# Second products of an expert's odd last bin: both k halves and both column halves side by side, one-hot transposes to match

## The chip, the cores and the metric

One core of a Trainium2 chip runs the program. The metric is device microseconds of one execution, the median of several runs. The engines that matter here are TensorE (its matmuls are "PE" in the profile, its weight loads "PEld"), VectorE (DVE), ScalarE (ACT) and the DMA queues: q1 carries data, q8 carries the program text of an engine.

## The reference, cut to what matters

A two-layer encoder for 256 tokens of width 1024. Its last stage is a mixture of eight experts, and the change lies there:

```
gate = sum(one_hot(top_idx, 8) * softmax(top_logit))      # two experts for each token
out = 0
for e in range(8):
    out += gate[:, e] * ((silu(x @ w1[e]) * (x @ w3[e])) @ w2[e])
```

w1 and w3 are 1024 x 3584, w2 is 3584 x 1024, all float32. The inputs are fixed, so the number of tokens of each expert is fixed too: 61, 32, 101, 73, 49, 83, 23, 90.

## The kernel before, in words

An expert's tokens are gathered into up to 128 columns, cut into **bins** of 32. The experts 0 to 7 so have 2, 1, 4, 3, 2, 3, 1 and 3 bins, 19 in all. TensorE works through the bins with a 32-column stationary operand, and so uses one of four column groups of the array; a product therefore goes to one **quarter** (32 partitions) of a PSUM tile, and four products that write four quarters run side by side.

The expert's weights come as 42 **blocks** of 1 MB, 128 x 2048 floats. Blocks 0 to 27 are the first products (w1, w3), blocks 28 to 41 the second products (w2): such a second block holds two k tiles (index `i`) of 128 rows by 1024 columns, the columns in two halves (`half`). Method `second(j)` (line 914) multiplies block 28 + j. Its inner `pair(m)` (line 919) does the bins 2m and 2m+1: for each i, each half and each bin rr one product of 512 columns into quarter 2 * half + rr of `py[m]`, 8 products in all, which add up over i:

```
for i in range(2):
    for half in range(2):
        for rr in range(2):
            g = 2 * half + rr
```

So a bin's two halves of the columns sit in two quarters, and a pair that has one bin only still does 8 products, 4 of them on a bin without tokens.

How many bins an expert has is known only on the chip. Before the experts, the counts are compared with 32.5, 64.5 and 96.5 and loaded into registers of TensorE alone (`sel`). `bins_over(n, some, none)` (line 841) is a branch on such a register; both branches are in the program, one after the other, and the other engines pass them with an unconditional branch. `second` calls `pair(0)`, then `bins_over(2, ...)` round `pair(1)`; where the second pair isn't there, a tiny matmul `mark` (line 824) takes its place. `quad` (line 851) does the first products in the same way, with a branch for each bin.

`where` (line 947) transposes the one-hot matrix of the expert's places, 16 small matmuls (line 952); `add` (line 967) multiplies these transposes with the second products and so brings the rows back to the tokens, in two column halves.

The order of the work is written out by hand in `moe` (lines 985 to 1039): for an expert the blocks 0 to 7, then the last two second blocks of the expert before, then blocks 8 to 23, second blocks 0 to 3, the gather for the next expert, blocks 24 to 27, and second blocks 4 to 11, with the transposes (`turn`, line 898) and `where` between. The blocks are fetched by SP's queue in this order into a ring of about 21 places, so that a block's transfer waits until TensorE has used the place's last block.

Of the kernel before, what the change touches and what calls it, by code (L numbers as in the profile page):

```python
# [21 lines left out]
D = 1024  # L22
# [49 lines left out]
def trunk(tc, A, out):  # L72
    nc = tc.nc
# [573 lines left out]
    def moe(xs, gb):  # L647
        with tc.tile_pool(name="moe", bufs=1, reuse_waits="tile") as ep:
# [48 lines left out]
            zero = ep.tile([128, 512], BF16, name="zero")  # L697
# [124 lines left out]
            def mark(ps):  # L822

                nc.tensor.matmul(ps[0:32, 0:1], zero[:, 0:32], zero[:, 0:1], start=True, stop=True)  # L824

            class Expert:
# [90 lines left out]
                def second(self, j):  # L917

                    w, q, c = self.w[28 + j], j // 4, j % 4

                    def pair(m):
                        for i in range(2):
                            for half in range(2):
                                for rr in range(2):
                                    g = 2 * half + rr
                                    if q < 3:
                                        h = self.h[q][m][:, rr, i, 32 * c:32 * c + 32]
                                    else:
                                        h = self.h[q][0][:, m, i, 32 * (2 * rr + c):32 * (2 * rr + c) + 32]
                                    nc.tensor.matmul(self.py[m][32 * g:32 * g + 32], h,  # L930
                                                     w[:, i * D + half * 512:i * D + half * 512 + 512],
                                                     start=j == 0 and i == 0, stop=j == 13 and i == 1)

                    def zeros():
                        if j:
                            mark(self.py[1])
                        else:
                            nc.tensor.matmul(self.py[1], zero[:, 0:128], zero, start=True, stop=True)

                    pair(0)  # L940
                    self.bins_over(2, lambda: pair(1), zeros)

                def where_places(self):
                    self.wtr = trp.tile([128, 2, 2, 128], F32, name="tr")

                def where(self):

                    for m in range(2):
                        for t in range(2):
                            for g in range(4):  # L950
                                r = 2 * m + g % 2
                                nc.tensor.matmul(self.wtr[32 * g:32 * g + 32, m, t], self.oh[:, t, 32 * r:32 * r + 32],
                                                 ident, start=True, stop=True)

                def wheres(self):
                    self.ohT = (xhp if self.inner else ep).tile([128, 2, 2, 128], F32R, name="ohT",
                                                                tag="xl" if self.inner else "ohT")
                    nc.scalar.activation(self.ohT, self.wtr, AF.Copy)
# [99 lines left out]
            with tc.manual_schedule():  # L1058
# [6 lines left out]
                for t in range(2):  # L1065
                    for h in range(2):
                        c = norms[t].finish(h)
# [11 lines left out]
    for l in range(DEPTH):  # L1079
        xs = mixer(l, xs, lambda l=l: load_gb(1 + 2 * l))  # L1080
        if l % 2 == 0:
            xs = ffn(xs, lambda: load_gb(2))
    moe(xs, lambda: load_gb(4))
    ctx.close()

# [145 lines left out]
```

## Time and profile before

| | us |
|---|---|
| median of three runs | 1604.64 (1604.07 to 1605.26) |
| the profiled execution, its own time | 1606.61 |
| its span, from the first to the last instruction | 1604.6 |
| experts, from their first product to the last | 672.6 to 1586 |
| PE busy over the span | 1539.1 (96%) |
| DVE, ACT busy over the span | 574.3 (36%), 427.7 (27%) |

The profiled execution has 2.0 us outside its span, and is 2.0 us slower than the median. Read PE's 96% with care: the matmuls of four quarters overlap, and the busy time of an engine that waits in the middle of such a group can look full. What the experts' stage is held up by is read from its waits, expert by expert.

The order in which TensorE's instructions stand, from the listing of the built program (x8 is eight products in a row; the program holds the branches one after the other). On TensorE, a second block before (L930 is `pair`, L824 `mark`; `s` is py, `raw` the block, `eh` the hidden values):

```order
L930 MATMUL s<-raw,eh 32x512 x8
L845 COMPARE_AND_BRANCH
L930 MATMUL s<-raw,eh 32x512 x8
L845 UNCONDITIONAL_BRANCH
L824 LDWEIGHTS zero
L824 MATMUL s<-zero 32x1
L845 UNCONDITIONAL_BRANCH
```

The second pair and the mark are the two ways of one branch, after a first pair that is always done.

### The profile page before, as it was taken

What the parts mean: (1) busy time and instruction counts of PE and PEld (TensorE: products, weight loads), DVE (VectorE), ACT (ScalarE), POOL (GpSimd) and SP (SyncE); (2) the same over time, 40 slices, a digit from 0 to 9 for tenths busy, and PEclk for the clock granted to TensorE, in tenths of its full rate; (3) what the DMA queues carried; (4) which work ended last, traced back from release to release, by engine and by line L of the source; (5) the groups of instructions that cost most, each with busy time, mean ns of one, the idle gap of its engine ahead of it and who ended that gap; (6) DMA issues with size and microseconds to landing.
All of it is one profiled execution on the core that took longest, in us unless ns stands there. A gap on an engine that the chain in (4) does not pass through costs nothing. (4 is left out here: it accounts for less than half of the span.)

```text
span 1604.6 us, 27197 instructions
## 1 busy us (share of the span) xinstructions
PE 1539.1 (96%) x11516; PEld 861.4 (54%) x11533; DVE 574.3 (36%) x1070; ACT 427.7 (27%) x704; POOL 28.7 (2%) x29
## 2 busy tenths in 40 slices
PE   8999999999999999899799999999999999999996
PEld 7687887888786877634232333433334343334332
DVE  7689576554676967510110100110010200210102
ACT  4556555444364666210010000000000100110001
POOL 1000000000010000000000000000000000000000
PEclk9999999999999999999899999999999999999998
DMA  8444546555454564799999999997999997999930
GB/s 348 152 138 158 190 157 221 184 189 193 161 187 165 180 247 161 282 419 418 417 419 420 419 420 350 369 342 273 345 418 419 419 414 281 401 419 419 419 127 29
DMA packets 66977, 468.95 MB, mean 292 GB/s; under 512 B 7552, under 2 KB 8192, under 8 KB 11264
## 3 DMA queue, kind: packets, MB, share of 16 engines
q1 hardware_dynamic: 66816, 466.55, 74.6%
q8 instruction: 131, 2.15, 0.5%
q14 instruction: 30, 0.25, 0.0%
HBM read 465.48 MB, written 1.05 MB: 291 GB/s over the span
## 5 line engine op out<-in xcount | busy, mean ns | idle before, releaser
L858 PE MATMUL mm<-raw,xe 128*32 128x512 f32 x4416 | 499.8, 598 | 20.2 <-issue 13.9
L171 PE MATMUL mm<-w,xh 128*128 128x512 f32 (+2 forms) x1184 | 313.7, 385 | 1.9 <-ACT xh L163 1.9
L858 PEld LDWEIGHTS mm<-raw,xe 128*32 128x32 f32 x4416 | 164.8, 110 | 267.0 <-issue 241.3
L930 PE MATMUL s<-raw,eh 128*32 128x512 f32 x2688 | 300.2, 595 | 6.3 <-DMA raw<-wmoe 4.6
L139 DVE TENSOR_TENSOR w<-raw,w 128x1024 fp32r<-128x1024 f32 (+1 forms) x198 | 238.4, 1208 | 135.4 <-ACT w L135 134.7
L135 ACT ACTIVATE w<-raw 128x1024 fp32r<-128x1024 f32 (+1 forms) x198 | 206.2, 1047 | 198.7 <-PE mm L171 172.6
L171 PEld LDWEIGHTS mm<-w,xh 128*128 128x128 f32 x1184 | 215.7, 189 | 45.7 <-ACT xh L163 3.6
L930 PEld LDWEIGHTS s<-raw,eh 128*32 128x32 f32 x2688 | 92.5, 110 | 175.9 <-issue 158.2
L171 PE MATMUL mm<-w,xl 128*128 128x512 f32 (+2 forms) x592 | 178.1, 384 | 0.6 <-DVE xl L164 0.6
L911 ACT ACTIVATE eh<-tr 128x512 f32<-128x512 f32 x32 | 19.1, 597 | 494.9 <-PE tr L901 494.9
L892 DVE TENSOR_TENSOR fs<-mm,fs 128x256 f32<-128x256 f32 x112 | 40.4, 416 | 284.0 <-ACT fs L891 283.9
L909 DVE COPY eh<-tr 128x512 f32<-128x512 f32 x24 | 16.6, 692 | 294.1 <-PE tr L901 294.1
L171 PEld LDWEIGHTS mm<-w,xl 128*128 128x128 f32 x592 | 107.9, 189 | 22.2 <-issue 1.5
L891 ACT ACTIVATE fs<-mm 128x256 f32<-128x256 f32 x112 | 34.9, 393 | 202.1 <-PE mm L858 175.5
L824 PEld LDWEIGHTS <-zero 128*32 128x32 bf16 x211 | 20.7, 98 | 80.3 <-issue 80.3
L978 DVE SCALAR_TENSOR_TENSOR acc<-tr,egate,acc 128x512 f32<-128x512 f32 x32 | 22.8, 749 | 106.1 <-PE tr L974 106.1
L520 DVE SCALAR_TENSOR_TENSOR ac<-ud,smc,ac 128x256 f32<-128x256 f32 x120 | 53.2, 479 | 0.7
L171 PE MATMUL mm<-xh,w 128*128 128x256 f32 x256 | 45.2, 289 | 0.0
L171 PE MATMUL mm<-w,hh 128*128 128x512 f32 x144 | 44.3, 389 | 0.0
L171 PEld LDWEIGHTS mm<-xh,w 128*128 128x128 f32 x256 | 36.3, 191 | 3.2 <-issue 3.0
L171 PE MATMUL mm<-w,yh 128*128 128x512 f32 x128 | 35.8, 401 | 0.0
L824 PE MATMUL mm<-zero 128*32 128x1 bf16 x159 | 26.8, 168 | 8.9 <-issue 8.9
(203 smaller groups left out, 1032.4 us busy)
## 6 DMA issues: line engine op xcount, KB each, us to landing
raw<-wmoe SPq DMA_DIRECT2D x334, 1024.0 KB, 19.8
raw<-wpre SPq DMA_DIRECT2D x95, 1024.0 KB, 4.9
gb<-lnp SPq DMA_DIRECT2D x5, 1024.0 KB, 6.0
raw<-wpre SPq DMA_DIRECT2D x4, 704.0 KB, 6.0
z<-biasB SPq DMA_DIRECT2D x8, 256.0 KB, 2.7
raw<-wmoe SPq DMA_DIRECT2D x4, 512.0 KB, 16.8
z<-cw SPq DMA_DIRECT2D x2, 640.0 KB, 6.7
x<-x SPq DMA_DIRECT2D x2, 512.0 KB, 3.9
```

The costliest lines, as they stand in the source:

```text
L135: nc.scalar.activation(self.w[h][0], raw[:, h * self.n:(h + 1) * self.n], AF.Copy)
L139: (eng or nc.vector).tensor_tensor(wl, raw[:, h * self.n:(h + 1) * self.n], f(wh), op=ALU.subtract)
L171: nc.tensor.matmul(ps, o[i], o[j], start=start and q == 0 and k == 0, stop=stop and q == 2 and k == n - 1)
L520: later.append(lambda c=c, k=k, w=w: nc.vector.scalar_tensor_tensor(ac[:, c], ud[:, c, k:k + S], w(k), ac[:, c], op0=ALU.mult, op1=ALU.add))
L824: nc.tensor.matmul(ps[0:32, 0:1], zero[:, 0:32], zero[:, 0:1], start=True, stop=True)
L858: nc.tensor.matmul(ps[bank][32 * g:32 * g + 32], self.xe[:, k, 32 * r:32 * r + 32], w[:, c0:c0 + 512], start=k == 0, stop=k == 7)
L891: nc.scalar.activation(s, ps[:, 0:256], AF.Silu)
L892: nc.vector.tensor_tensor(s, ps[:, 256:512], s, op=ALU.mult)
L909: nc.vector.tensor_copy(h, tr)
L911: nc.scalar.activation(h, tr, AF.Copy)
L930: nc.tensor.matmul(self.py[m][32 * g:32 * g + 32], h, w[:, i * D + half * 512:i * D + half * 512 + 512], start=j == 0 and i == 0, stop=j = ...
L978: nc.vector.scalar_tensor_tensor(acc[t][:, c], ps[h], gate[:, t, self.e:self.e + 1], acc[t][:, c], op0=ALU.mult, op1=ALU.add, accum_out=su ...
```

## The change

`pair` stays for two bins. A new `one(m)` does a single bin: its two k halves and two column halves go to the four quarters (quarter 2 * half + i), 4 products instead of 8, and the sum over the two k halves is left to `add`. For that, `where` puts the one-hot of the single bin at both quarters of a half, by a branch. `second` now branches three ways deep: one bin, two, three, or four.

```diff
@@ -918,39 +918,59 @@
 
                     w, q, c = self.w[28 + j], j // 4, j % 4
 
+                    def product(m, rr, i, half, g):
+                        if q < 3:
+                            h = self.h[q][m][:, rr, i, 32 * c:32 * c + 32]
+                        else:
+                            h = self.h[q][0][:, m, i, 32 * (2 * rr + c):32 * (2 * rr + c) + 32]
+                        return [self.py[m][32 * g:32 * g + 32], h, w[:, i * D + half * 512:i * D + half * 512 + 512]]
+
                     def pair(m):
                         for i in range(2):
                             for half in range(2):
                                 for rr in range(2):
-                                    g = 2 * half + rr
-                                    if q < 3:
-                                        h = self.h[q][m][:, rr, i, 32 * c:32 * c + 32]
-                                    else:
-                                        h = self.h[q][0][:, m, i, 32 * (2 * rr + c):32 * (2 * rr + c) + 32]
-                                    nc.tensor.matmul(self.py[m][32 * g:32 * g + 32], h,
-                                                     w[:, i * D + half * 512:i * D + half * 512 + 512],
+                                    nc.tensor.matmul(*product(m, rr, i, half, 2 * half + rr),
                                                      start=j == 0 and i == 0, stop=j == 13 and i == 1)
 
-                    def zeros():
+                    def one(m):
+                        for half in range(2):
+                            for i in range(2):
+                                nc.tensor.matmul(*product(m, 0, i, half, 2 * half + i), start=j == 0, stop=j == 13)
+
+                    def none(m):
                         if j:
-                            mark(self.py[1])
+                            mark(self.py[m])
                         else:
-                            nc.tensor.matmul(self.py[1], zero[:, 0:128], zero, start=True, stop=True)
-
-                    pair(0)
-                    self.bins_over(2, lambda: pair(1), zeros)
+                            nc.tensor.matmul(self.py[m], zero[:, 0:128], zero, start=True, stop=True)
+
+                    def both():
+                        pair(0)
+                        self.bins_over(2, third, lambda: none(1))
+
+                    def third():
+                        self.bins_over(3, lambda: pair(1), lambda: one(1))
+
+                    def single():
+                        one(0)
+                        if j == 0:
+                            none(1)
+
+                    self.bins_over(1, both, single)
 
                 def where_places(self):
                     self.wtr = trp.tile([128, 2, 2, 128], F32, name="tr")
 
                 def where(self):
 
-                    for m in range(2):
+                    def quarters(m, rr, r):
                         for t in range(2):
-                            for g in range(4):
-                                r = 2 * m + g % 2
+                            for g in (rr, 2 + rr):
                                 nc.tensor.matmul(self.wtr[32 * g:32 * g + 32, m, t], self.oh[:, t, 32 * r:32 * r + 32],
                                                  ident, start=True, stop=True)
+
+                    for m in range(2):
+                        quarters(m, 0, 2 * m)
+                        self.bins_over(2 * m + 1, lambda: quarters(m, 1, 2 * m + 1), lambda: quarters(m, 1, 2 * m))
 
                 def wheres(self):
                     self.ohT = (xhp if self.inner else ep).tile([128, 2, 2, 128], F32R, name="ohT",
```

The same place on TensorE in the changed program (L932 is `pair`, L938 `one`, L824 `mark`):

```order
L845 COMPARE_AND_BRANCH
L932 MATMUL s<-raw,eh 32x512 x8
L845 COMPARE_AND_BRANCH x2
L932 MATMUL s<-raw,eh 32x512 x8
L845 UNCONDITIONAL_BRANCH
L938 MATMUL s<-raw,eh 32x512 x4
L845 UNCONDITIONAL_BRANCH
L824 LDWEIGHTS zero
L824 MATMUL s<-zero 32x1
L845 UNCONDITIONAL_BRANCH
L938 MATMUL s<-raw,eh 32x512 x4
L845 UNCONDITIONAL_BRANCH
```

24 products stand in the program for each second block where 16 stood, and nine branches and mark instructions where there were five; the first branch stands ahead of all products. And the one-hot transposes on TensorE, 16 in a row before, in the changed program (L968):

```order
L901 MATMUL tr<-ident,fs 128x128 x4
L968 MATMUL tr<-ident,oh 32x128 x4
L845 COMPARE_AND_BRANCH
L968 MATMUL tr<-ident,oh 32x128 x4
L845 UNCONDITIONAL_BRANCH
L968 MATMUL tr<-ident,oh 32x128 x4
L845 UNCONDITIONAL_BRANCH
L968 MATMUL tr<-ident,oh 32x128 x4
L845 COMPARE_AND_BRANCH
```

As many are done, and half as many again stand there, with two branches.

## Rows read from the trace of the kernel before

**Rows 1.** Windows, one per expert (0 to 7), cut at its first product.

```profile
core 0: us, PE busy (x) PEld busy (x) DVE busy (x) ACT busy (x) POOL busy (x), PEclk, DMA share, GB/s
672.60:756.20 83.60, 81.36 (x774) 32.62 (x780) 9.22 (x27) 11.87 (x25) 0.00 (x0) 1.00 1.01 419
756.20:846.90 90.70, 74.08 (x643) 26.37 (x640) 12.04 (x30) 8.64 (x22) 0.00 (x0) 0.94 1.01 418
846.90:1000.40 153.50, 152.34 (x1423) 53.61 (x1426) 12.13 (x30) 8.75 (x22) 0.00 (x0) 1.00 0.99 405
1000.40:1138.60 138.20, 136.28 (x1285) 52.89 (x1284) 12.23 (x30) 8.86 (x22) 0.00 (x0) 1.00 0.86 319
1138.60:1230.50 91.90, 90.23 (x859) 37.50 (x857) 12.22 (x30) 8.86 (x22) 0.00 (x0) 1.00 1.01 412
1230.50:1365.40 134.90, 132.98 (x1259) 51.35 (x1257) 12.13 (x30) 8.75 (x22) 0.00 (x0) 1.00 0.94 376
1365.40:1447.60 82.20, 75.06 (x667) 29.20 (x665) 12.13 (x30) 8.75 (x22) 0.00 (x0) 0.96 1.00 411
1447.60:1586.00 138.40, 136.26 (x1290) 49.96 (x1287) 11.84 (x28) 8.79 (x23) 0.00 (x0) 1.00 0.65 270
```

**Rows 2.** PE's waits in expert 1, 756 to 847 us: total, times, longest.

```profile
PE mm L858 <- DMA raw<-wmoe: 4.7, 6, 1.5
PE s L930 <- DMA raw<-wmoe: 4.6, 7, 1.6
```

**Rows 3.** PE's waits from 847 to 1586 us, experts 2 to 7.

```profile
PE mm L858 <- issue: 9.7, 15, 1.4
PE mm L824 <- issue: 3.1, 1, 3.1
...
PE mm L858 <- DMA raw<-wmoe: 1.1, 3, 0.6
```

**Rows 4.** PE in order of time, expert 3 (three bins): four second blocks, then the gather.

```profile
1076.98 13.94 PE L930 MATMUL s<-raw,eh 128*32 128x512 f32 x128
1090.85 1.38 PE L759 MATMUL tr<-oh,x 128*128 128x128 f32 x10
```

**Rows 5.** PE in order of time, expert 4 (two bins): second blocks with their marks.

```profile
1223.59 1.90 PE L930 MATMUL s<-raw,eh 128*32 128x512 f32 x16
1225.31 0.17 PE L824 MATMUL s<-zero 128*32 128x1 bf16 x1
```

**Rows 6.** DMA queue q8 in: whole span; expert 1; expert 5; 758:787; 1375:1411.

```profile
q8 instruction: 131, 2.15, 0.5%
q8 instruction: 13, 0.21, 1.0%
q8 instruction: 13, 0.21, 0.6%
q8 instruction: 5, 0.08, 1.1%
q8 instruction: 6, 0.10, 1.1%
```

**Rows 7.** PE in order of time, expert 6 (one bin): first blocks, then a second block.

```profile
1388.71 1.13 PE L858 MATMUL mm<-raw,xe 128*32 128x512 f32 x8
1389.58 0.17 PE L824 MATMUL mm<-zero 128*32 128x1 bf16 x1
...
1407.54 0.19 PE L824 MATMUL mm<-zero 128*32 128x1 bf16 x1 [3.12 <-issue]
1407.55 1.93 PE L858 MATMUL mm<-raw,xe 128*32 128x512 f32 x8
...
1411.31 2.98 PE L930 MATMUL s<-raw,eh 128*32 128x512 f32 x16
```

**Rows 8.** PE's branches (ns: shortest, median, longest): expert 6, then expert 5.

```profile
L845 PEldq COMPARE_BRANCH  x45: 70/208/5233, 1367.1 to 1447.8; - x45
L845 PEldq COMPARE_BRANCH  x129: 65/169/449, 1231.0 to 1364.6; - x129
```

## The prediction

> **What bounds the kernel now.** I read the experts' stage expert by expert, then the waits, then single stretches. The table by expert [rows 1] shows what a bin costs in time: the experts with one or two bins take 82 to 92 us, those with three 135 to 138, the one with four 153.5. Weights come at 418 or 419 GB/s, the highest rate there is, in experts 0 and 1; in experts 2, 3 and 5 they come at 405, 319 and 376: there TensorE frees the places too late, and the queue stands still. So I ask for each expert whether TensorE waits for weights. In expert 1 it does, 9.3 us in all [rows 2], and its end at 846.9 is set by the transfer. From there to the last product at 1586 it waits for weights 1.1 us in three pieces [rows 3]: all 739 us belong to TensorE. What shortens a product after 847 shortens the kernel, and what shortens one before is lost in a wait.
>
> One more limit shows in these rows. In experts 2 to 7 PE waits at least 12.8 us for "issue" [rows 3], which is no data: its own instructions aren't there. The instruction queue brings 131 packets of 2.15 MB, so 16.4 KB each, and in each expert 13, whether it has one bin or three [rows 6]: the text of all branches is loaded, taken or not. By the listing an expert's text is some 3,350 instructions (a float32 product counts four: two weight loads, two matmuls), so 13 packets carry 257 each. Where a bin's work is short, the packets come as fast as they can: five in 29 us in expert 1, six in 36 us in expert 6 [rows 6], 5.8 to 6.0 us each. There a branch of expert 6 lasts 5.2 us, against 0.45 at most in expert 5 [rows 8], and PE stands for 3.1 us [rows 7]. I take **5.9 us a packet** as the price of text.
>
> **The change part by part.**
>
> *Three bins (experts 3, 5, 7).* Four second blocks of 32 matmuls take 13.87 us from their first to the gather behind them [rows 4]: 0.108 us a matmul. A block loses 4 products, 8 matmuls: 0.867 us, and an expert with 14 blocks 12.1 us. Do the four quarters still overlap if each streams its own weights and its own k tile? The first products do that already, four column ranges into four quarters, and eight matmuls start 0.87 us before what follows [rows 7]; so yes. Is the text there in time? A second block grows from 69 to 105 instructions (24 products instead of 16, nine other instructions instead of five): 105/257 of 5.9 us is 2.4 us, just below the 2.6 us that 24 matmuls take. Only the block with the one-hot transposes, whose text reaches 215 instructions, 4.9 us, against some 4.2 us of work, falls behind. I take 11.3 us an expert: **-34 us**, with 10.5 and 12.1 as bounds.
>
> *Expert 6 (one bin).* PE gets 0.87 us of work for a second block where it had 1.73, half of it. Without the text that were another 12.1 us. But the expert's text becomes 3,890 instructions, 15.1 packets, 89.3 us at 5.9; the expert takes 82.2 now [rows 1]. Its stretch from the first second block, 1411.3 [rows 7], to 1447.6 lasts 36.3 us and holds 1,260 instructions, 4.9 packets, 29 us: covered. Changed it holds 1,690, 6.6 packets, 38.8 us: 2.5 us longer. The first blocks ahead of it wait for packets already, so nothing is in hand when it begins, and the bound of the whole expert is the nearest: **+7 us**, between +2.5 and +9 (6.0 us a packet).
>
> *Expert 4 (two bins).* The work is the same, 1.72 us a block [rows 5], against 2.4 us of text. The same stretch of 1,260 instructions, some 35.3 us, becomes 38.8: +3.5; the whole, 15.1 packets, is 89.3 us against 91.9. The wait falls in the stretch and the rest is too slow to give it back; its last two blocks add half a us: **+4 us**, between 0 and +6.
>
> *Experts 0 and 1.* Expert 0 (two bins) gets the same 3.5 us. Expert 1 (one bin) then needs 89.3 us for its text where it now takes 90.7 with the waits for weights: expert 2 starts **2 us** later, between 0 and 5. Its saved products gain nothing, they would only lengthen the waits of [rows 2]. Two of its second blocks stand in expert 2 and cost 2.4 us of text each instead of 1.72: **+1 us**, 0 to 1.4.
>
> *The clock.* After the 3.1 us of standing, eight matmuls took 1.93 us and the next second block 2.98 instead of 1.90 [rows 5, 7]: half speed, the 1.2 of the two levels 1.2 and 2.4 GHz; the granted clock is 0.94 and 0.96 in the experts with one bin and 1.00 in all others [rows 1]. That stall cost 2 us more. With more waits and less work in experts 1 and 6, the next expert can begin so: **+2 us**, 0 to 5.
>
> *At nothing.* As many one-hot transposes run as before, and the branches are passed by PE's sequencer while the array works: in expert 5, where nothing waits for text, 129 branches have a median of 0.17 us [rows 8] beside blocks of 2.6 to 3.5 us. If that cover goes, it is text that is missing, which is costed above. `add`, the ACT and DVE work and the order of the fetches stay. The ring can't become the limit: 405, 319 and 376 of 419 GB/s in experts 2, 3 and 5 are 5, 33 and 14 us of idle transfer [rows 1], more than TensorE can gain.
>
> The sum is -34 + 7 + 4 + 2 + 1 + 2 = **-18 us**: the profiled execution's 1606.6 would be 1588.6. The median of the runs stands 2.0 us below that execution, at 1604.64, so I predict **1587**. All bounds on the good side give -33.8, on the bad side -5.
>
> For the price of text the Trainium skill has a rule that speaks the other way. On the page "Runtime: NRT & Kernel Launch", section "Instruction fetch mechanics", it says that instructions are loaded in blocks of 16 KiB while the block before is worked on, and that crossing into a new one is mostly hidden. By that, experts 4 and 6 would lose nothing. The trace agrees with the size of a packet, 16.4 KB, and not with the hiding where bins are few: 3.1 us of standing in one wait [rows 7]. The same section says that a taken branch to text not yet loaded stalls until it is there, which fits the branch of 5.2 us [rows 8].
>
> **The rivals.**
>
> *Text stays hidden.* If the longer blocks are loaded in time, the three-bin experts give 36.3, expert 6 another 12.1 and the last two blocks of expert 1, which stand behind 847, 1.7: -50 us, **1555**. For it speaks that experts 2, 3, 5 and 7 run without waits for text; against it that the packets of experts 1 and 6 already come at their highest rate [rows 6]. It is also what the Trainium skill's page "Runtime: NRT & Kernel Launch" would have, by its hidden crossings. 7 in 100.
>
> *Text costs more than it looks* (slower). If a packet takes 6.5 us when more are asked for beside a saturated weight queue, an expert with one or two bins needs 15.1 x 6.5 = 98.2 us: expert 6 loses 16, expert 4 6.3, experts 0 and 1 together some 15.1 (6.6 packets in place of 35.3 us, then 98.2 in place of 90.7), expert 2 2, the clock 2, and the three-bin blocks (2.66 us of text) still give 32: +9 us, **1614**. Each 0.1 us more a packet costs some 5 us over these experts, so from -18 at 5.9 the point of no gain lies near 6.25 us. For it: single gaps of expert 6 exceed the mean; against it: two stretches agree on 5.8 and 6.0. 9 in 100.
>
> *The four quarters do not overlap* with four k and column combinations, so the change does not do what it says: then a group of four takes as long as eight, the three-bin experts give nothing and the text still costs 16: **1621**. Against it stand the first products. 2 in 100.
>
> **How the numbers follow.** The forecast has the remaining 82 in 100; its own bounds are 1570.8 to 1599.6. I give 1570 to 1602: the rival with hidden text lies below, the two slow ones above, and a part of the forecast's upper end is kept for prices of text up to 6.2. What a measurement of this kernel can tell from no change is about 0.2%, 3.2 us. Faster by more than that is below 1601.4: the hidden text and nearly all of the forecast, 0.84. Slower is above 1607.8: the two slow rivals less a small part, 0.09. Between: 0.07.
>
> **What would show it.** In the profile after: L930's rows split into `pair` and `one`, 1,568 and 560 matmuls instead of 2,688 together; expert 3 and 5 some 10 us shorter in the table by expert (two of an expert's second blocks stand in the next one's window), expert 6 longer than 82.2 although it does less work, with "issue" as its wait; 15 packets of q8 in each expert and about 148 in all; no wait for weights behind expert 1. The prediction is wrong if expert 6 gets shorter (text hidden), if expert 4 takes over 98 us (text dearer), or if a three-bin second block still takes 3.4 us.

## The result and the profile after

The changed kernel takes 1586.88 us (1584.54 to 1590.49, four runs) where the kernel before took 1604.95 (1604.07 to 1605.26) on the same chip: ratio 0.9894, interval 0.9883 to 0.9906, so 18.1 us faster. The forecast was 1587. The profiled execution is the slowest of the four, 1590.49 with a span of 1588.4; its span is 16.2 us shorter than the one of before, and that is the difference taken apart here.

From the page of the changed kernel: the second products (L932 is `pair`, L938 `one`) and the text queue. Columns: busy, mean ns of one | idle before, and what ended most of it.

```profile
span 1588.4 us, 26211 instructions
...
q8 instruction: 148, 2.42, 0.6%
...
L932 PE MATMUL s<-raw,eh 128*32 128x512 f32 x1568 | 185.2, 595 | 3.0 <-issue 2.8
...
L938 PE MATMUL s<-raw,eh 128*32 128x512 f32 x560 | 83.8, 643 | 11.6 <-issue 11.6
```

560 matmuls fewer, 17 packets of text more (131 before, [rows 6]), and idle time ahead of L938 that is "issue", no data. The windows by expert say where that counts.

Windows of the changed kernel, one per expert (0 to 7), cut at its first product as in [rows 1].

```profile
core 0: us, PE busy (x) PEld busy (x) DVE busy (x) ACT busy (x) POOL busy (x), PEclk, DMA share, GB/s
673.30:759.00 85.70, 82.08 (x772) 34.16 (x778) 9.21 (x27) 12.25 (x25) 0.00 (x0) 1.00 1.01 419
759.00:851.90 92.90, 67.63 (x536) 24.15 (x533) 12.13 (x30) 8.75 (x22) 0.00 (x0) 0.93 1.01 418
851.90:1006.00 154.10, 151.02 (x1408) 52.48 (x1404) 12.13 (x30) 8.74 (x22) 0.00 (x0) 1.00 0.96 389
1006.00:1134.60 128.60, 126.54 (x1192) 52.11 (x1191) 12.12 (x30) 8.74 (x22) 0.00 (x0) 1.00 0.89 342
1134.60:1227.80 93.20, 89.12 (x840) 37.56 (x838) 12.13 (x30) 8.75 (x22) 0.00 (x0) 1.00 1.01 415
1227.80:1353.80 126.00, 123.89 (x1160) 49.77 (x1159) 12.12 (x30) 8.75 (x22) 0.00 (x0) 1.00 0.98 396
1353.80:1442.50 88.70, 69.59 (x546) 25.74 (x543) 12.03 (x30) 8.64 (x22) 0.00 (x0) 0.92 1.01 416
1442.50:1568.60 126.10, 123.69 (x1157) 50.07 (x1152) 11.14 (x27) 8.15 (x21) 0.00 (x0) 1.00 0.67 276
```

Against [rows 1], experts 3, 5 and 7 are 9.6, 8.9 and 12.3 us shorter (12.2 by unrounded starts, and so used below), and expert 6 is 6.5 longer although PE has 5.5 us less work in it. Experts 0, 1 and 4 are 1.3 to 2.2 us longer.

The timeline of PE in the changed kernel shows the loss at the end of expert 1, the gain in expert 3 (four second blocks, then the gather) and the loss at the end of expert 6. Columns: start, length, operation, [idle before].

```profile
848.56 3.50 PE L938 MATMUL s<-raw,eh 128*32 128x512 f32 x16 [3.55 <-issue]
...
1082.60 1.92 PE L932 MATMUL s<-raw,eh 128*32 128x512 f32 x16
1084.34 1.04 PE L938 MATMUL s<-raw,eh 128*32 128x512 f32 x8
1085.20 1.90 PE L932 MATMUL s<-raw,eh 128*32 128x512 f32 x16
...
1093.04 3.17 PE L759 MATMUL tr<-oh,x 128*128 128x128 f32 x26
...
1438.23 4.48 PE L938 MATMUL s<-raw,eh 128*32 128x512 f32 x24 [2.44 <-issue]
1442.53 3.67 PE L858 MATMUL mm<-raw,xe 128*32 128x512 f32 x24
```

Four blocks last 10.44 us, from 1082.60 to 1093.04, against 13.87 [rows 4]: 0.858 us less a block, and the eight matmuls of `one` take 0.86 us to what follows (1084.34 to the next block at 1085.20). They overlap as those of `pair` do, of which sixteen take 1.74. Behind 2.44 us of standing, 24 matmuls take 4.30 us to what follows (1438.23 to 1442.53), where the 24 of a block in expert 3 take 2.60; the granted clock falls to 0.62 in a window from 1438.2 to 1441.0.

PE's waits in the changed kernel (total, times, longest), first in expert 1 (759 to 851.9), then in expert 6 (1353.8 to 1442.5):

```profile
PE mm L824 <- issue: 11.0, 5, 2.9
PE s L938 <- issue: 7.0, 3, 3.6
PE mm L858 <- issue: 2.5, 3, 1.2
PE mm L866 <- issue: 2.4, 1, 2.4
PE tr L968 <- issue: 2.2, 1, 2.2
...
PE mm L824 <- issue: 6.2, 3, 2.4
PE mm L858 <- issue: 5.2, 4, 3.0
PE s L938 <- issue: 4.4, 3, 2.4
PE tr L968 <- issue: 2.5, 1, 2.5
PE tr L759 <- issue: 0.8, 1, 0.8
```

And its branches in expert 6 (ns: shortest, median, longest):

```profile
L845 PEldq COMPARE_BRANCH  x49: 65/208/5433, 1355.6 to 1439.4; - x49
```

Expert 1 waited 9.3 us for weights [rows 2]. Now it never does; it waits 25.1 us for its own text, and text sets its end. Expert 6 has 19.1 us of such waits, branches of up to 5.4 us as before [rows 8], and 15 packets in its window, where an expert had some 13 [rows 6]. No weights are late there: by the trace each of expert 6's blocks lands at least 23 us before its first product.

### The profile page after: what moved, and what is told of

Read it like the earlier page. It is cut to its first block, busy times and chain, and to the rows that moved or that the text cites. A ratio compares the mean times of both kernels' runs of the same rounds, so it can differ in the third digit from the quotient of the medians.

```text
span 1588.4 us, 26211 instructions
## 1 busy us (share of the span) xinstructions
PE 1495.2 (94%) x10932; PEld 855.6 (54%) x10947; DVE 574.0 (36%) x1070; ACT 427.4 (27%) x704; POOL 28.8 (2%) x29
## 5 line engine op out<-in xcount | busy, mean ns | idle before, releaser
L858 PE MATMUL mm<-raw,xe 128*32 128x512 f32 x4416 | 500.9, 597 | 20.7 <-issue 18.3
L858 PEld LDWEIGHTS mm<-raw,xe 128*32 128x32 f32 x4416 | 163.5, 110 | 274.7 <-issue 256.7
L932 PE MATMUL s<-raw,eh 128*32 128x512 f32 x1568 | 185.2, 595 | 3.0 <-issue 2.8
L911 ACT ACTIVATE eh<-tr 128x512 f32<-128x512 f32 x32 | 19.1, 597 | 480.3 <-PE tr L901 480.3
L932 PEld LDWEIGHTS s<-raw,eh 128*32 128x32 f32 x1568 | 62.8, 110 | 93.5 <-issue 81.2
L938 PE MATMUL s<-raw,eh 128*32 128x512 f32 x560 | 83.8, 643 | 11.6 <-issue 11.6
L824 PEld LDWEIGHTS <-zero 128*32 128x32 bf16 x185 | 18.1, 98 | 79.8 <-issue 79.6
L938 PEld LDWEIGHTS s<-raw,eh 128*32 128x32 f32 x560 | 23.2, 115 | 51.4 <-issue 47.8
L824 PE MATMUL mm<-zero 128*32 128x1 bf16 x159 | 26.8, 169 | 17.3 <-issue 17.3
## 6 DMA issues: line engine op xcount, KB each, us to landing
raw<-wmoe SPq DMA_DIRECT2D x334, 1024.0 KB, 19.1
```

The costliest lines, as they stand in the source:

```text
L858: nc.tensor.matmul(ps[bank][32 * g:32 * g + 32], self.xe[:, k, 32 * r:32 * r + 32], w[:, c0:c0 + 512], start=k == 0, stop=k == 7)
L911: nc.scalar.activation(h, tr, AF.Copy)
L932: nc.tensor.matmul(*product(m, rr, i, half, 2 * half + rr), start=j == 0 and i == 0, stop=j == 13 and i == 1)
L938: nc.tensor.matmul(*product(m, 0, i, half, 2 * half + i), start=j == 0, stop=j == 13)
```

## The experiments

The theory: PE's text comes at some 5.9 us a packet beside a full weight queue, so what stands in the program costs, whether it is executed or not. Its rivals: text is hidden, or the branches and the new products themselves are what costs.

**Text alone.** The kernel before with eight or sixteen more products in the program for each second block. They stand on a branch that is never taken (the registers hold 3 at most; the bound that the code declares for them is raised to 7), so every expert does the same products as before. In the experts with three or four bins PE passes one more branch a block (848 in all instead of 792), in the others none.

```diff
-                    self.bins_over(2, lambda: pair(1), zeros)
+                    self.bins_over(2, lambda: self.bins_over(6, lambda: pair(1), lambda: pair(1)), zeros)
```

In the second kernel the branch that is not taken holds `pair(1)` twice.

> The kernel before, with eight products more in the program text of each second block, behind a branch that is never taken; the same products run. Text theory (an expert lasts as long as the longer of its work and its text, some 5.9 us for a packet of 257 instructions; the text of all experts grows by some 15 packets): 12 to 22 us slower than before, expert 6 by 5 to 8 us, expert 4 by 2 to 4, expert 2 starts 4 to 7 us later, experts 3, 5 and 7 within 2 us. Rival (only what runs counts; what experts 4 and 6 lost after the change comes from its branch ahead of the products or from the order of the single bin's products): within 1 us of before.

> The same with sixteen dead products in each second block, some 29 packets of text more. Text theory: 45 to 60 us slower than before, so more than twice dead8, since experts 0, 1, 4 and 6 are then bound by text throughout: expert 6 by 14 to 18 us, expert 4 by 8 to 11. Rival: within 1 us of before.

Eight: 1613.63 us, ratio 1.0060 (1.0043 to 1.0076), 9.4 us slower. Sixteen: 1656.47, ratio 1.0324 (1.0303 to 1.0344), 52 us slower. Expert 6 with sixteen, by its window (columns as above), and then by its first two waits:

```profile
1401.40:1497.80 96.40, 78.81 (x670) 29.32 (x665) 12.13 (x30) 8.75 (x22) 0.00 (x0) 0.95 1.01 412
```

```profile
PE s L824 <- issue: 6.3, 5, 2.2
PE mm L824 <- issue: 5.2, 3, 2.0
```

The window holds 16 packets. Products that never run cost 14.2 us in expert 6, 13.8 in expert 0 and 11.9 in expert 4 (8 to 11 expected), 1.6 in expert 5, and nothing in experts 3 and 7 (0.0 and -0.1): experts with three bins have work enough to cover nearly all of it. Hidden text is refuted, and so are the branches as the cause, as the experts that lose most pass none more. The nine us of the smaller kernel lie below the 12 expected, and so do its parts: expert 2 starts 1.2 us later (4 to 7 expected) and expert 6 loses 3.0 (5 to 8). It has 146 packets, 1.9 an expert more than before, and those 3.0 us are half of one packet; from there to sixteen (160 packets, 1.75 an expert more) it lost another 11.2, 6.4 us a packet. So a first packet or so is free, and what comes behind it has the full price.

**One part of the change alone.** The three-bin part: `third` and the branch in `where` for the fourth bin stay, the outermost branch goes.

```diff
-                    self.bins_over(1, both, single)
+                    both()
...
-                        self.bins_over(2 * m + 1, lambda: quarters(m, 1, 2 * m + 1), lambda: quarters(m, 1, 2 * m))
+                        if m == 0:
+                            quarters(m, 1, 1)
+                        else:
+                            self.bins_over(3, lambda: quarters(1, 1, 3), lambda: quarters(1, 1, 2))
```

> The change for three bins alone: two bins or one do the pair as before, so expert 6 does twice the second products of the changed kernel, and 20 products stand in the text of a block in place of 24. Text theory: 28 to 33 us faster than before, so 10 to 15 faster than the changed kernel, with expert 6 at 82 to 86 us and expert 4 at 90 to 92. Rival (only what runs counts): slower than the changed kernel by the products of expert 6, 10 to 12 us.

And the one-bin part: `single` stays, a second pair is always `pair(1)`.

```diff
-                        self.bins_over(2, third, lambda: none(1))
+                        self.bins_over(2, lambda: pair(1), lambda: none(1))
...
-                        self.bins_over(2 * m + 1, lambda: quarters(m, 1, 2 * m + 1), lambda: quarters(m, 1, 2 * m))
+                        if m:
+                            quarters(1, 1, 3)
+                        else:
+                            self.bins_over(1, lambda: quarters(0, 1, 1), lambda: quarters(0, 1, 0))
```

> The change for one bin alone: experts 1 and 6 do half their second products, three bins do two pairs as before; 20 products in the text of a block. Text theory: 0 to 4 us slower than before, expert 6 at 82 to 86 us although it does 12 us less work. Rival: 12 to 14 us faster than before, expert 6 near 72 us.

Three bins alone: **1572.72 us** (1572.28 to 1573.43), ratio 0.9803 (0.9787 to 0.9819): 31.5 us faster than before, and 14 faster than the whole change. One bin alone: 1606.58, ratio 1.0013 (1.0004 to 1.0023), no gain. Both totals lie where the text theory had them; expert 6 came out about a microsecond below its 82 to 86 in both. Expert 6 by its window in the two, three bins alone first; each window holds 13 packets:

```profile
1344.60:1425.50 80.90, 74.12 (x652) 29.53 (x650) 12.22 (x30) 8.86 (x22) 0.00 (x0) 0.96 1.01 414
```

```profile
1367.20:1448.30 81.10, 64.79 (x562) 24.42 (x559) 12.13 (x30) 8.75 (x22) 0.00 (x0) 0.96 1.00 409
```

With one bin alone PE has 10.3 us less to do in expert 6 than before (64.79 against 75.06, [rows 1]) and the window is 1.1 us shorter: its work doesn't set its length, its text does. Each part alone puts 20 products in the program for a second block and brings 139 or 140 packets, one an expert more than before, and that one is free. Together they put 24 there, 148 packets, two an expert more. The parts alone add up to -31.5 + 2.3 = -29.2 us, the change gives -18.1: the 11 us between come with the second packet.

**The packet's price.** The changed kernel with every fourth weight block fetched, and used for itself and the three blocks behind it. It leaves out three quarters of the experts' weights; all instructions of the products are done.

```diff
+            order = [o for o in order if o[1] % 4 == 0]
...
+                        elif n % 4:
+                            self.w[n] = self.w[n - n % 4]
```

> The changed kernel with one weight block in four fetched and used for all four, so a quarter of the weight traffic; the products then use wrong weights, and TensorE's work and text stay. It tells what sets the price of a packet. If packets are slow because they queue behind the weights: expert 6 falls from 88 to 89 us to between 60 and 75, expert 1 likewise. If the price is that of a packet by itself: expert 6 stays at 86 to 90 and expert 1 falls to the same.

One run: 1529.61 us. Windows of experts 1, 4 and 6, then PE's waits in expert 6:

```profile
756.00:822.00 66.00, 59.57 (x533) 23.05 (x530) 12.13 (x30) 8.75 (x22) 0.00 (x0) 1.00 0.51 178
...
1102.00:1194.50 92.50, 89.27 (x842) 38.19 (x838) 12.14 (x30) 8.75 (x22) 0.00 (x0) 1.00 0.36 127
...
1319.40:1383.10 63.70, 59.30 (x550) 24.81 (x547) 12.04 (x30) 8.64 (x22) 0.00 (x0) 1.00 0.25 86
```

```profile
PE mm L825 <- issue: 1.7, 1, 1.7
PE mm L861 <- issue: 1.4, 2, 1.2
PE s L941 <- issue: 1.3, 1, 1.3
```

With the DMA engines at a share of 0.25 instead of 1.01, expert 6 falls from 88.7 to 63.7 us, and at 0.51 expert 1 from 92.9 to 66.0, with the same text. 14 packets come in expert 6's 63.7 us, at most 4.6 us each, and PE is nearly the bound (59.3 of 63.7). By the starts of the packets in the traces, no two are closer than 5.6 us in experts 1, 4 and 6 of the changed kernel, and the closest in this run's expert 6 are 3.1 us apart. So 5.9 us is not the packet's own price: it is what a packet takes behind weights. The granted clock is 1.00 in every expert, so the half speed of before and after came from those waits too. Expert 4 hardly gains (92.5 against 93.2): its wait for text is another kind, below.

From expert 2 to the end PE still has these waits with the quiet data queue (L861 is here what L858 is in the other kernels):

```profile
PE mm L861 <- issue: 10.0, 17, 1.4
```

That is as much as the 9.7 us of [rows 3]: a stop of 1.16 us comes in experts 0 to 6 and one of 1.4 in expert 7, here as in the kernel before, behind the same transposes; in expert 6 of the kernel before the trace lays it to VectorE. So most of these waits are no text that queues behind weights.

**Less text in the same program.** Two products that `pair(1)` and `one(1)` have in common written once, ahead of the branch (18 products for a second block instead of 20), on three bins alone, in all second blocks but the last.

```diff
-                        self.bins_over(3, lambda: pair(1), lambda: one(1))
+                        shared()
+                        self.bins_over(3, rest_of_pair, rest_of_one)
```

> three_only with the two products that a full pair and an odd bin have in common written once ahead of the third branch: 18 products in the text of a block in place of 20, some 3 packets less over all experts; the same products run. Text theory: 0 to 2 us faster than three_only, in experts 4 and 6. Rival (what runs counts, and a branch in the middle of a group of four quarters breaks their overlap): 5 us or more slower than three_only, in experts 3, 5 and 7.

1573.61 us (1571.97 to 1576.02), ratio 0.9816 (0.9803 to 0.9830): not to be told from three bins alone, and the rival's 5 us are not there. PE's waits for second blocks in expert 4, first with three bins alone, then here:

```profile
PE s L932 <- issue: 1.9, 2, 1.7
```

```profile
PE s L932 <- issue: 0.3, 1, 0.3
```

Two changes stand behind the equal sum. Expert 4 is 1.9 us shorter (90.2 against 92.1), as expected, its single stop of 1.7 us gone; expert 6 is 1.9 longer (82.8 against 80.9), with 9.7 us of waits at its marks instead of 5.0. So less text won nothing in sum; what lengthened expert 6 stays open.

**Without marks.** Three bins alone, with no `mark` in a branch of a bin that isn't there, in `quad` and in `second`.

```diff
-                        if j:
-                            mark(self.py[m])
-                        else:
+                        if j == 0:
```

> three_only without the marks (the tiny matmul in place of a bin or pair that isn't there, from the second block of an accumulation on), so two instructions fewer for each branch level: some 2 packets less text over all experts. Text theory: 1 to 4 us faster than three_only, mostly in experts 1 and 6. If text is no limit there: the same within 1 us.

1653.50 us, ratio 1.0310 (1.0296 to 1.0324): 50 us slower than before, some 80 slower than with the marks, a clear miss. The waits of PE over the span, then its branches' line, then a piece of expert 3's timeline:

```profile
PE mm L858 <- PEq L845: 52.1, 127, 2.3
...
PE tr L899 <- PEq L845: 7.5, 22, 1.0
PE s L930 <- PEq L845: 7.0, 37, 0.4
PE tr L988 <- PEq L845: 4.7, 11, 0.5
```

```profile
L845 PEldq EVENT_SEMAPHORE  x211: 51/51/51, 677.2 to 1579.5; - x106
```

```profile
1064.72 2.33 PE L858 MATMUL mm<-raw,xe 128*32 128x512 f32 x20
1067.50 2.78 PE L858 MATMUL mm<-raw,xe 128*32 128x512 f32 x24 [0.45 <-PEq L845]
1070.81 1.20 PE L988 MATMUL tr<-ey,ohT 64*128 64x512 f32 x8 [0.52 <-PEq L845]
```

211 instructions on the branches' line are there that no kernel with marks has, as many as three bins alone has marks. The array stands behind the branches' line, 0.45 and 0.52 us here, 71.3 us in the 197 waits of the four rows, 0.36 each. I read it so that the sequencer raises the semaphore itself where no matmul of the branch can, and lets the array run empty first; the rows show the instructions and the standing, not that reason. A mark takes 0.17 us beside other work [rows 5], and by that reading the semaphore's count is what it buys.

## Why the prediction was right

Term by term, in us of the profiled span. Two of an expert's second blocks stand in the next one's window; for three bins they give 1.7 us there (in the changed kernel's expert 4, PE's timeline has them from 1149.21 to 1154.15, 4.94 us; before from 1153.23 to 1159.89, 6.66). So 1.7 is moved from experts 4 and 6 to 3 and 5.

| term | forecast | measured | from |
|---|---|---|---|
| experts 3, 5, 7 | -34 | -34.1 | -9.6 - 1.7, -8.9 - 1.7, -12.2 |
| expert 6 | +7 | +8.2 | +6.5 + 1.7 |
| expert 4 | +4 | +3.1 | +1.4 + 1.7 |
| expert 2 starts later | +2 | +5.0 | 846.9 to 851.9 |
| its two blocks of expert 1 | +1 | +0.6 | 153.5 to 154.1 |
| clock | +2 | in the rows above | |
| behind the last product | 0 | +1.1 | 18.7 to 19.8 |
| sum | -18 | -16.1 | span -16.2 |

The median's 1586.88 against 1587 is closer than the terms are: single terms are off by up to 3 us, some each way, and the four runs spread over 6 us. To meet it within 0.1 us was luck.

*Three bins.* The step is shown: four quarters with their own weights and k tiles overlap, 0.858 us a block against 0.867 forecast. The forecast took that from the first products, whose four products share a k tile and a bin, so the run shows more than they did. The bound of 12.1 an expert is reached where text is free: three bins alone give 12.0, 12.1 and 11.7. In the whole change experts 3 and 7 give 11.3 and 12.2, and expert 5 10.6; the forecast's 11.3 stood for the block with the transposes, whose text was to fall behind. It does: of the 0.7 us that expert 3 lacks, 0.6 are one stop two blocks behind the transposes (eight matmuls of `one` at 1127.95 take 1.46 us to the next block instead of 0.86), and with a quiet data queue that stop is gone. Expert 5 lacks 0.5 there too, and 1.0 at its start, mostly in and ahead of expert 4's two blocks. Expert 7's 12.2 is not the three bins alone: expert 6's last two blocks in it are 1.0 shorter (3.43 to 2.38), and its own first eight blocks, begun at the low clock, take 0.8 longer.

*Expert 6.* 15.1 packets at 5.9 were to make 89.3; the window has 15 packets and 88.7 us. The price and the count are right, and the two kernels with text alone show the mechanism without the change's products. The row is 1.2 off because 89.3 bounds the whole window, with expert 5's two blocks in it: the -34 counts their 1.7 as gained, and in a window that text sets they gain nothing. What the forecast had wrong is the picture that every packet has that price: 13 packets took 82.2 us, 6.3 each, so the kernel before still had about one packet in hand.

*Expert 4.* +3.1 against +4, by another way than forecast. Its waits for "issue" went from 1.7 to 4.0 us, in single waits of 0.9 us at the one-hot transposes and 1.5 behind them, and with a quiet data queue 3.2 us of them stay. So it is no queue of packets that falls behind, as the forecast had it, but single stops. Its longest branch takes 3.6 us, where before it took 1.0, which a branch to text not there would give; but with three bins alone the stop of 1.7 us stands beside branches of 1.1 us at most. With two products written once it is gone, which a quiet data queue didn't bring about, so it hangs on the text itself; in which way stays open. The 1.0 us at expert 5's start come on top, where the forecast had half a microsecond.

*Expert 2's start* is the term that was mis-sized: +5.0 for +2, the end of its bounds. Expert 1 took 92.9 us where 89.3 were forecast: 16 packets fell into its window and 13 into expert 0's, where 15.1 each were forecast, and 16 at 5.8 are 92.8. Expert 0 lost 2.1 instead of 3.5. The stage began 0.7 later, and that is no more than kernels with nothing changed ahead of it show (672.1 to 673.8 over the kernels with one, two or no part of it). The 1.1 us behind the last product stays open.

*Clock.* It is in the terms above, as said. Expert 6's last blocks show it: 24 matmuls in 4.30 us that take 2.60 at full clock, 1.7 us for one stall; and ahead of expert 2 16 in 3.50 that take 1.92, 1.6 us. The forecast's 2 were for both together.

*The waits for "issue".* The forecast read 12.8 us of them in experts 2 to 7 as text [rows 3]. For the 9.7 of them at L858 there are 10.0 with a quiet data queue, as shown, so most of these were no late text. No term of the sum uses the 12.8.

*The rivals.* Hidden text is refuted by the never-taken products. A dearer packet isn't seen: experts 1 and 6 give 5.8 and 5.9, counted by their windows, and 6.1 from their first packet's start to their last one's; both lie below the 6.25 of no gain. The rule of the Trainium skill's page "Runtime: NRT & Kernel Launch", section "Instruction fetch mechanics", that crossings into a new block are mostly hidden, describes the kernel with a quiet data queue (4.4 us of waits in expert 6) and not the one with the weights (19.1 us; 1.16 us of each is the stop that experts 0 to 6 share). Its other rule, that a taken branch to text not loaded stalls, agrees with branches of 5.4 us in expert 6.

*The best version found* is three bins alone, 1572.72 us: it beats both kernels.

## What to carry to other kernels

In this kernel the branch not taken is paid for in text. Where branches are taken at run time, count the instructions of all branches against the time of the shortest path, and price them by the packets of the text queue beside the transfers of that very stretch. Two special cases that each fit can fail together, so try each part of such a change alone; here the part that saved most work on paper per block (half of it) saved nothing, because its experts were waiting for text or weights. Ask what bounds the path you shorten before you shorten it.

## What the hardware showed that was not expected

- The same 16.4 KB packets of text take 5.9 us each while the DMA engines are at a share of 1.01, and at most 4.6 us at 0.25; 25 us of an expert's 88.7 hang on that.
- An empty branch is dearer than one with a tiny matmul: 211 semaphore instructions of the sequencer came with 71 us of standing in 197 waits and a kernel 80 us slower, where marks of 0.17 us run beside other work.
